# Half row factors and q copies tied behind weight splits, state-space steps in another order, the last feed-forward tile half by half

## The chip, the cores and the metric

The kernel runs on one core of one Trainium2 chip. The metric is the device time of one execution in microseconds (us), smaller is better. TensorE (PE in the rows, its weight loads PEld), VectorE (DVE), ScalarE (ACT), GpSimd (POOL) and SyncE (SP) each work through their own instruction list in order; what one needs from another it waits for at a semaphore.

## The reference

Two layers of a hybrid block on x of 256 tokens by 1024 features, all in fp32. Cut to what matters here:

```
h = rmsnorm(x, attn_norm_g)
gm_u, gm_v, ssm_z, ssm_xbc, ssm_dt, q, k, v, gates = split(h @ w_in)
y_a = gelu(gm_u) * (causal w_s applied to rmsnorm(gelu(gm_v)))          # spatial gating
y_b = rmsnorm((ssd_scan(conv(ssm_xbc), softplus(ssm_dt)) ) * silu(ssm_z))  # 16 heads of 64, chunks of 128
y_c = rmsnorm(softmax(q1 k1) v - lam * softmax(q2 k2) v)                 # 4 heads, two score maps each
g = sigmoid(gates)                                                       # three branches
x = x + (g_a*(y_a@w_a) + g_b*(y_b@w_b) + g_c*(y_c@w_c)) @ w_out
up = causal_conv3(rmsnorm(x) @ w_up);  gate, val = split(up)             # width 2816 each
x = x + (silu(gate) * val) @ w_down
```

In the scan a chunk's output is decay-masked scores times inputs within the chunk, plus what the state before it carries in.

## The kernel before

**Weights.** All weights come as one stream of 1 MB blocks over SP's queue into `raw` (3 buffers). `AHEAD` = 4 halves ahead of their use each half of a block (128x1024) is split in two: ScalarE copies it, rounded, into `whi` (L232), and VectorE writes what the rounding lost into `wlo` (L235, five buffers of each). A product is three matmuls (`mm3`, L277 to L279): high by high, high by low, low by high. `tok_group` makes an output of 256 tokens by 512 columns with matmuls of 512 columns, `feat_half` and the down projection with 256.

**Order.** The main line calls the products one after the other: q, k, the convolution inputs, v, z, the spatial branch, then for each branch the gate product and the branch product (`g_a`, `b_a`, `g_c`, `b_c`, `g_b`, `b_b`), the out projection, and 22 tile pairs of the feed-forward block with their down projection (blocks of two tiles). Small work runs beside it as generators that `tick()` steps a little after every half block, each at a rate: `norm_factors` (the row factors of an rmsnorm: squares, a sum over features by matmul `ss`, a power on POOL `r`, then `rh`, half of it, for the gates' tanh, and a row form `row`), `ssd` (rate `SSD_RATE`) and the attention. The Tile scheduler then lays the instructions of each engine in one list by priority; `tc.high_priority` moves work ahead, and `tc.issue_after(ins)` keeps work behind a given instruction.

**State-space steps.** `ssd` goes through a table, `order`. For chunk i and head group g, `decay(i, g)` makes the decay matrix in place of the buffer `seg` (eight Relu on ScalarE at L857, one Exp at L864), `masked(i, g)` multiplies it with scores and mask (VectorE, L870); `carried(g)` makes `ce` (Exp on ScalarE L846, a product on VectorE L847); `products(q)` is 24 small matmuls into `y` (L884, L886) which read two `seg` and one `ce`; `gated(q)` and `parts(q)` turn `y` into the operand of `b_b`; `factor` sums its squares (`yss`). `seg`, `ce` and other wide tiles share `NS4` = 18 buffers.

**Attention.** For a head: `sc` (scores, PE), maximum (VectorE), Exp (ScalarE, `pe`), combination (VectorE), `wt` (transposes on PE), `wT` (their copy by ScalarE, L660), `po` (PE).

**End of the feed-forward block.** `gather(j)` adds the two parts of an up tile (ScalarE L1092, VectorE L1093), `hidden(j)` does the causal convolution (L747, L752), silu (L1111), the product (L1112) and the split into `act` (ScalarE L345 high part, VectorE L347 low part). Tiles 20 and 21 feed the last down block, in which the accumulators `acc` get finished and x is updated.

Of the kernel before, what the change touches and what calls it, by code (L numbers as in the profile page):

```python
# [26 lines left out]
NFT = FFN // P  # L27
# [3 lines left out]

MIX = ("q", "k", "x4", "x5", "v", "x0", "x1", "z0", "z1", "x2", "x3", "z2", "z3", "g", "u0", "u1")

NS4, NS2, NWB, AHEAD = 18, 7, 5, 4
HP = 200


# [2 lines left out]
ROW_WAIT = 4  # L40
WARM = 11
SEG_ACT = 8
XT_RATE, SSD_RATE, ATT_RATE = 0.8, 0.95, 1.45
ATTN_IN_RATE, SSD_IN_RATE, GATE_RATE = 0.6, 0.5, 0.7


# [83 lines left out]
def block_kernel(ctx: ExitStack, tc: tile.TileContext, x, wstream, wdt, rows, prol, pcols, gains, gmw, consts, out):  # L130
    nc = tc.nc
# [5 lines left out]
    sm = ctx.enter_context(tc.tile_pool(name="sm", bufs=2))  # L137
# [9 lines left out]
    def s2(name, shape, dt=F32):  # L147
        return sm.tile(shape, dt, tag="s2", name=name, bufs=NS2)
# [51 lines left out]
    stream = {"i": 0, "raw": None}  # L200
    ready = deque()

    def load_half():
        i, hf = divmod(stream["i"], 2)
        parts = 1
        if hf == 0:
            raw = wpool.tile([P, BLK], F32, tag="raw", name=f"raw{i}", bufs=3)
            if i == 0:

                for q in range(4):  # L210
                    cs = slice(q * 512, (q + 1) * 512)
# [12 lines left out]
        src = stream["raw"][:, hf * HB : (hf + 1) * HB]
        hi = wpool.tile([P, HB], F32R, tag="whi", name=f"whi{i}_{hf}", bufs=NWB)
        lo = wpool.tile([P, HB], F32R, tag="wlo", name=f"wlo{i}_{hf}", bufs=NWB)
        for q in range(parts):
            cs = slice(q * HB // parts, (q + 1) * HB // parts)
            if i == 0:
                for k in (4 * hf + 2 * q, 4 * hf + 2 * q + 1):  # L230
                    scaled_tile(k, 0, *hT0)
            split = nc.scalar.activation(hi[:, cs], src[:, cs], AF.Copy)  # L232
            if i < 2:
                stream["first"] = split.ins
            nc.vector.tensor_tensor(lo[:, cs], src[:, cs], hi[:, cs].bitcast(F32), op=ALU.subtract)  # L235
        stream["i"] += 1
        ready.append((hi, lo))

# [144 lines left out]
    def norm_factors(name, res, later):  # L383


        tot = None
        for b in range(4):
            sq = s2(f"{name}_sq{b}", [P, 2, S])
            with tc.issue_after(stream["first"]):
                nc.scalar.activation(sq, x_sb[:, 2 * b : 2 * b + 2, :], AF.Square)  # L390
            if b:
                nc.vector.tensor_tensor(sq, sq, tot, op=ALU.add)
            tot = sq
        nc.vector.tensor_tensor(tot[:, 0, :], tot[:, 0, :], tot[:, 1, :], op=ALU.add)
        yield
        yield
        t = ps(f"{name}_ss")
        for i in range(2):
            nc.tensor.matmul(t[:, i : i + 1], tot[:, 0, i * P : (i + 1) * P], ones, start=True, stop=True)
        ss = sm.tile([P, 2], F32, tag="nss", name=f"{name}_s", bufs=2)  # L400
        nc.vector.tensor_copy(ss, t[:, 0:2])
        r = rsqrt_mean(ss, 2, 1.0 / D, f"{name}_r")
        rh = sm.tile([P, 2], F32, tag="rhalf", name=f"{name}_rh", bufs=2)
        nc.vector.tensor_scalar(rh, r[:, 0:2], 0.5, None, op0=ALU.mult)
        res.update(r=r, rh=rh)
        for _ in range(later):
            yield
        t2 = ps(f"{name}_rb")
        for i in range(2):
            nc.tensor.matmul(  # L410
                t2[:, i * P : (i + 1) * P], r[:, i : i + 1].to_broadcast([P, P]), ident, start=True, stop=True
            )
        row = sm.tile([P, S], F32, tag="rrow", name=f"{name}_row", bufs=1)
        nc.vector.tensor_copy(row, t2[:, 0:S])
        res.update(row=row)

    def hT_pair(name):
        return (
# [27 lines left out]
    for l in range(L):  # L446
# [3 lines left out]
        nf = {}  # L450
# [5 lines left out]
        def evac_qk(c0):  # L456
            def f(i, o):
                nc.scalar.activation(qk[i][:, c0 : c0 + 512], o, AF.Identity, scale=nf["r"][:, i : i + 1])

            return f  # L460

        nf_side = add_side(norm_factors(f"an{l}", nf, ROW_WAIT), 1)
        q_out = {}
        tok_group(f"q{l}", h_act, 8, q_out.__setitem__)
        r_in, rh_in = nf["r"], nf["rh"]

        def q_evac():
            for i in range(2):
                evac_qk(0)(i, q_out[i])

        pc, rw, gw, sub_g, ws = lc or layer_constants(l)

# [356 lines left out]
        def ssd():  # L829
# [88 lines left out]
            def factor():  # L918
# [7 lines left out]
                ry.append(rsqrt_mean(ss, 2, 1.0 / D, f"ry{l}"))  # L926

            order = (
                (decay, 0, 0), (masked, 0, 0), (carried, 0), (decay, 1, 0), (masked, 1, 0), (products, 0),
                (decay, 0, 1), (gated, 0), (products, 1), (masked, 0, 1), (parts, 0), (gated, 1), (carried, 1),  # L930
                (decay, 1, 1), (parts, 1), (masked, 1, 1), (products, 2), None, (gated, 2), (products, 3),
                (parts, 2), (gated, 3), None, (parts, 3), None, (factor,),
            )
            for e in order:
                if e:
# [55 lines left out]
        def branch(nm, y_act, nk, first, before, between=None):  # L991
            gts = []
            for n in range(2):
                gt = s4(f"gt{l}_{nm}_{n}", [P, 2, 512])
                gts.append(gt)
                tok_group(
                    f"g{l}_{nm}_{n}", h_act, 8,
                    lambda i, o: nc.scalar.activation(gt[:, i, :], o, AF.Tanh, scale=rh_in[:, i : i + 1]),
                )
            finish(before)  # L1000
            for n in range(2):
                cs = slice(512 * n, 512 * n + 512)
# [12 lines left out]
                tok_group(f"b{l}_{nm}_{n}", y_act, nk, evac, between if n == 1 else None)
# [22 lines left out]
        for kh in range(2):  # L1038
            for t2 in range(4):
                whi, wlo = next_half()  # L1040
                for m in range(2):
                    t = 2 * t2 + m
                    o = po[t2][:, m * S : (m + 1) * S]
# [16 lines left out]
        act, outs, us, ys, hm = {}, {}, {}, {}, []  # L1060
# [20 lines left out]
                    )  # L1081
                yield

        def gather(j):

            o = outs.pop(j)
            if j < MERGE:
                us[j] = normed(o[0], nff["row"], f"fu{l}_{j}")
                return
            us[j] = u = s2(f"fu{l}_{j}", [P, 2, S])  # L1090
            for m in range(2):
                nc.scalar.activation(u[:, m, :], o[m][:, S : 2 * S], AF.Copy)  # L1092
                nc.vector.tensor_tensor(u[:, m, :], o[m][:, 0:S], u[:, m, :], op=ALU.add)  # L1093

        def hidden(j):

            if j % 2 == 0:
                ys[0] = s4(f"fy{l}_{j}", [P, 2, 2, S])
                act["tile"] = s4(f"act{l}_{j}", [P, 4, S], F32R)
            u, y, a = us.pop(j), ys[0], act["tile"]  # L1100
            for m in range(2):
                t = 2 * j + m
                conv(u[:, m, :], y[:, m, j % 2, :], PC_FW + 3 * t, PC_FB + t, 3, pc)
            act[j] = (a[:, j % 2, :], a[:, 2 + j % 2, :])
            if j >= NFT - 2:
                js = slice(j % 2, j % 2 + 1)
            elif j % 2 == 1:
                js = slice(0, 2)
            else:
                return  # L1110
            nc.scalar.activation(y[:, 0, js, :], y[:, 0, js, :], AF.Silu)  # L1111
            nc.vector.tensor_tensor(y[:, 1, js, :], y[:, 0, js, :], y[:, 1, js, :], op=ALU.mult)  # L1112
            split_T(a[:, js, :], a[:, 2 + js.start : 2 + js.stop, :], y[:, 1, js, :])
# [5 lines left out]
        for kind, j in ffn_order():  # L1119
            if kind == "down" and not acc:  # L1120
                acc.extend(ps(f"acc{l}_{b}") for b in range(4))
            if kind == "up":
# [20 lines left out]
                if j:  # L1143
                    hidden(j - 1)
                if j == NFT - 1:
                    gather(j)
                    hidden(j)
            elif j < NFT // 2 - 1:
                for kk in range(2):
                    half = next_half()  # L1150
# [106 lines left out]
```

## Time and profile before

| what | value |
|---|---|
| time, median of 3 runs | 949.3 us (948.8 to 950.59) |
| the profiled execution | 949.31 us, of which the span is 947.5 us |
| PE busy | 935.9 us, 99% of the span |
| PEld, DVE, ACT, POOL busy | 89%, 77%, 63%, 4% |
| granted clock of TensorE | 0.999 of full speed |
| moved by DMA | 171.70 MB, 181 GB/s in the mean |

The profiled execution is within 0.01 us of the median, so terms read from its rows can be taken off the median as they are. A busy PE is not one at its peak: matmuls are pipelined, each is drawn some 0.39 us long where they start 0.23 us apart. So what a wait costs is read from start to start.

### The profile page before, as it was taken

To read this page: it belongs to the slowest core of one execution; us is meant where nothing else is said; L and a number is where in the kernel's file an instruction comes from. 1 tells how busy PE (TensorE), PEld (TensorE's weight loads), DVE (VectorE), ACT (ScalarE), POOL (GpSimd) and SP (SyncE) were. 2 spreads that over 40 slices of the span, in tenths; PEclk is the share of its full clock that TensorE was granted. 3 is DMA by queue.
4 is the path that set the end of the run, shared out by engine and by line. 5 is a ranking of instruction groups with operands and counts; after the bars stand their busy time and mean duration, and the time that the engine had idled before them with its cause. 6 is when DMAs were issued, how large, how long until landed. Compare 5 with 4: busy or idle time off the path is not lost.

```text
span 947.5 us, 15508 instructions
## 1 busy us (share of the span) xinstructions
PE 935.9 (99%) x6179; PEld 840.4 (89%) x6179; DVE 726.7 (77%) x1126; ACT 595.0 (63%) x924; POOL 37.2 (4%) x44
## 2 busy tenths in 40 slices
PE   8999999999999999999999999999999999999998
PEld 5899987888899999999989998878888999999997
DVE  6798668876568987877778974878856789787775
ACT  6575588854456856666667655878544567566663
POOL 1020010010000000000001000101000000000000
PEclk9999999999999999999999999999999999999999
DMA  9645473544644555555544555734455545455541
GB/s 335 245 172 178 177 265 131 178 152 174 208 173 152 204 184 178 178 185 193 189 177 146 179 178 167 255 127 162 148 204 183 178 169 188 178 179 186 196 152 45
DMA packets 29143, 171.70 MB, mean 181 GB/s; under 512 B 5232, under 2 KB 6544, under 8 KB 9616
## 3 DMA queue, kind: packets, MB, share of 16 engines
q1 hardware_dynamic: 27712, 166.48, 49.7%
q0 software_dynamic: 1216, 4.23, 1.5%
q8 instruction: 48, 0.79, 0.3%
q14 instruction: 23, 0.19, 0.1%
q10 hardware_dynamic: 144, 0.02, 0.0%
HBM read 169.63 MB, written 1.08 MB: 180 GB/s over the span
## 4 chain that ended last, share of the span: by engine, by line
PE 89%; ACT 5%; DVE 4%; DMA 1%; issue 1%; POOL 0%; SPq 0%; ACTq 0%; POOLq 0%
PE up L298 10%; PE up L299 5%; PE acc L278 4%; PE acc L277 4%; PE acc L279 4%; PE xbc L279 2%; PE xbc L278 2%; PE xbc L277 2%; PE up L277 2%; PE up L278 2%; PE up L279 2%; ACT whi L232 2%; DVE wlo L235 2%; PE wo L278 2%; PE z L279 2%; PE z L277 2%
## 5 line engine op out<-in xcount | busy, mean ns | idle before, releaser
L235 DVE TENSOR_TENSOR wlo<-raw,whi 128x1024 fp32r<-128x1024 f32 (+1 forms) x310 | 376.8, 1220 | 134.6 <-ACT whi L232 134.0
L232 ACT ACTIVATE whi<-raw 128x1024 fp32r<-128x1024 f32 (+1 forms) x310 | 324.2, 1050 | 242.5 <-PE up L302 37.2
L298 PE MATMUL up<-hm,whi 128*128 128x512 f32 x420 | 150.2, 396 | 0.0
L299 PE MATMUL up<-hm,wlo 128*128 128x256 f32 x420 | 117.8, 280 | 0.0
L278 PE MATMUL acc<-act,whi 128*128 128x256 f32 x352 | 99.3, 283 | 0.6 <-DVE act L347 0.6
L279 PE MATMUL acc<-act,wlo 128*128 128x256 f32 x352 | 99.1, 283 | 0.0
L277 PE MATMUL acc<-act,whi 128*128 128x256 f32 x352 | 98.3, 284 | 0.3 <-ACT act L345 0.3
L298 PEld LDWEIGHTS up<-hm,whi 128*128 128x128 f32 x420 | 79.0, 188 | 16.3
L752 DVE SCALAR_TENSOR_TENSOR fy<-fu,pc,fy 128x254 f32<-128x254 f32 (+1 forms) x176 | 80.8, 481 | 12.3 <-ACT fy L747 10.7
L299 PEld LDWEIGHTS up<-hm,wlo 128*128 128x128 f32 x420 | 79.4, 189 | 2.0
L747 ACT ACTIVATE fy<-fu,pc 128x256 f32<-128x256 f32 x88 | 51.1, 593 | 36.6 <-DVE fu L1093 32.1
L278 PEld LDWEIGHTS acc<-act,whi 128*128 128x128 f32 x352 | 67.3, 191 | 1.5 <-DVE act L347 0.8
L277 PEld LDWEIGHTS acc<-act,whi 128*128 128x128 f32 x352 | 66.6, 191 | 0.8 <-ACT act L345 0.7
L279 PEld LDWEIGHTS acc<-act,wlo 128*128 128x128 f32 x352 | 67.3, 191 | 0.0
L277 PE MATMUL up<-f_hi,whi 128*128 128x256 f32 x224 | 63.7, 284 | 0.0
L278 PE MATMUL up<-f_lo,whi 128*128 128x256 f32 x224 | 63.4, 283 | 0.0
L279 PE MATMUL up<-f_hi,wlo 128*128 128x256 f32 x224 | 63.4, 283 | 0.0
L277 PE MATMUL xbc<-h_hi,whi 128*128 128x256 f32 x192 | 55.7, 290 | 0.0
L279 PE MATMUL xbc<-h_hi,wlo 128*128 128x256 f32 x192 | 54.3, 283 | 0.0
L278 PE MATMUL xbc<-h_lo,whi 128*128 128x256 f32 x192 | 54.3, 283 | 0.0
L278 PEld LDWEIGHTS up<-f_lo,whi 128*128 128x128 f32 x224 | 43.0, 192 | 0.0
L279 PEld LDWEIGHTS up<-f_hi,wlo 128*128 128x128 f32 x224 | 43.0, 192 | 0.0
(312 smaller groups left out, 2212.3 us busy)
## 6 DMA issues: line engine op xcount, KB each, us to landing
raw<-in_wstream SPq DMA_DIRECT2D x152, 1024.0 KB, 4.8
seg<-scr POOLq DMA_DIRECT2D x8, 512.0 KB, 6.7
rows<-in_rows SPq DMA_DIRECT2D x2, 648.0 KB, 5.8
x_sb<-in_x SPq DMA_DIRECT2D x4, 256.0 KB, 4.7
raw<-in_wstream SPq DMA_DIRECT2D x4, 256.0 KB, 4.8
raw<-in_wstream SPq DMA_DIRECT2D x2, 512.0 KB, 6.6
out_x<-x_sb SPq DMA_DIRECT2D x8, 128.0 KB, 1.8
gmw<-in_gmw SPq DMA_DIRECT2D x2, 256.0 KB, 5.6
```

Of the source, the lines that this page charges most:

```text
L232: split = nc.scalar.activation(hi[:, cs], src[:, cs], AF.Copy)
L235: nc.vector.tensor_tensor(lo[:, cs], src[:, cs], hi[:, cs].bitcast(F32), op=ALU.subtract)
L277: nc.tensor.matmul(o, a_hi, b_hi, start=start, stop=False)
L278: nc.tensor.matmul(o, a_hi, b_lo, start=False, stop=False)
L279: nc.tensor.matmul(o, a_lo, b_hi, start=False, stop=stop)
L298: nc.tensor.matmul(o, whi[:, ks], hk.rearrange("p a t -> p (a t)"), start=k == 0, stop=False)
L299: nc.tensor.matmul(o_a, a_lo, b_hi, start=False, stop=False)
L747: nc.scalar.activation(y, u, AF.Identity, bias=pcl[:, bcol : bcol + 1], scale=pcl[:, wcol + taps - 1 : wcol + taps])
L752: nc.vector.scalar_tensor_tensor(y[:, d:], u[:, : S - d], pcl[:, w : w + 1], y[:, d:], op0=ALU.mult, op1=ALU.add)
```

## The change

The half row factor `rh` is made at the end of `norm_factors`, after the row form, and issued after the latest `wlo` of that moment (`stream["low"]`); the two copies of the q product out of PSUM are issued after the latest `whi` (`stream["last"]`). The table of state-space steps is put in another order, its rate is lowered, and the wide tiles get a nineteenth buffer. The last feed-forward tile is gathered half by half inside `hidden`, and this call stands in a block of high priority.

```
-NS4, NS2, NWB, AHEAD = 18, 7, 5, 4
+NS4, NS2, NWB, AHEAD = 19, 7, 5, 4
-XT_RATE, SSD_RATE, ATT_RATE = 0.8, 0.95, 1.45
+XT_RATE, SSD_RATE, ATT_RATE = 0.8, 0.85, 1.45
...
             split = nc.scalar.activation(hi[:, cs], src[:, cs], AF.Copy)
+            stream["last"] = split.ins
...
-            nc.vector.tensor_tensor(lo[:, cs], src[:, cs], hi[:, cs].bitcast(F32), op=ALU.subtract)
+            low = nc.vector.tensor_tensor(lo[:, cs], src[:, cs], hi[:, cs].bitcast(F32), op=ALU.subtract)
+            stream["low"] = low.ins
...
         r = rsqrt_mean(ss, 2, 1.0 / D, f"{name}_r")
-        rh = sm.tile([P, 2], F32, tag="rhalf", name=f"{name}_rh", bufs=2)
-        nc.vector.tensor_scalar(rh, r[:, 0:2], 0.5, None, op0=ALU.mult)
-        res.update(r=r, rh=rh)
+        res.update(r=r)
...
         nc.vector.tensor_copy(row, t2[:, 0:S])
-        res.update(row=row)
+        rh = sm.tile([P, 2], F32, tag="rhalf", name=f"{name}_rh", bufs=2)
+        with tc.issue_after(stream["low"]):
+            nc.vector.tensor_scalar(rh, r[:, 0:2], 0.5, None, op0=ALU.mult)
+        res.update(row=row, rh=rh)
...
         def q_evac():
-            for i in range(2):
-                evac_qk(0)(i, q_out[i])
+
+            with tc.issue_after(stream["last"]):
+                for i in range(2):
+                    evac_qk(0)(i, q_out[i])
...
             order = (
-                (decay, 0, 0), (masked, 0, 0), (carried, 0), (decay, 1, 0), (masked, 1, 0), (products, 0),
...
+                (decay, 0, 0), (masked, 0, 0), (carried, 0), (decay, 1, 0), (masked, 1, 0), (decay, 0, 1),
+                (products, 0), (masked, 0, 1), (carried, 1), (gated, 0), (products, 1), (decay, 1, 1), (gated, 1),
+                (masked, 1, 1), (parts, 0), (parts, 1), (products, 2), None, (gated, 2), (products, 3), (parts, 2),
+                (gated, 3), (parts, 3), (factor,),
             )
...
-        def gather(j):
+        def gather(j, ms=(0, 1)):
...
-            u, y, a = us.pop(j), ys[0], act["tile"]
+            u, y, a = us.get(j), ys[0], act["tile"]
             for m in range(2):
+                if j == NFT - 1:
+                    gather(j, (m,))
+                    u = us[j]
...
                 if j == NFT - 1:
-                    gather(j)
-                    hidden(j)
+
+                    with tc.high_priority(HP):
+                        hidden(j)
```

How the lists of the engines change is shown at three places. The lists of SP and POOL stay as they are.

**Start of layer 0, VectorE** (`an0_ss` is the sum for the row factors, `an0_rp` its power from POOL, `an0_rh` the half factor, `wlo2_0` the low part of the first half block of the k product). Before:

```order
L401 COPY an0_s_228<-an0_ss_225 128x2
L404 TENSOR_SCALAR an0_rh_234<-an0_rp_232 128x2
L235 TENSOR_TENSOR wlo2_0_164<-raw2_161,whi2_0_163 128x1024
L235 TENSOR_TENSOR wlo2_1_192<-raw2_161,whi2_1_191 128x1024
L235 TENSOR_TENSOR wlo3_0_210<-raw3_207,whi3_0_209 128x1024
```

And with the change:

```order
L403 COPY an0_s_228<-an0_ss_225 128x2
L236 TENSOR_TENSOR wlo2_0_164<-raw2_161,whi2_0_163 128x1024
L236 TENSOR_TENSOR wlo2_1_192<-raw2_161,whi2_1_191 128x1024
L236 TENSOR_TENSOR wlo3_0_210<-raw3_207,whi3_0_209 128x1024
L236 TENSOR_TENSOR wlo3_1_235<-raw3_207,whi3_1_234 128x1024
```

The half factor no longer stands ahead of `wlo2_0`; it now comes after `wlo5_0`, fourteen rows further on.

**The same place, ScalarE** (`qk0_0` and `qk0_1` are the copies of the q product). Before:

```order
L232 ACTIVATE whi2_1_191<-raw2_161 128x1024
L458 ACTIVATE qk0_0_107<-q0_0_110,an0_rp_232 128x512
L458 ACTIVATE qk0_1_108<-q0_1_111,an0_rp_232 128x512
L232 ACTIVATE whi3_0_209<-raw3_207 128x1024
L232 ACTIVATE whi3_1_236<-raw3_207 128x1024
L232 ACTIVATE whi4_0_287<-raw4_285 128x1024
L232 ACTIVATE whi4_1_316<-raw4_285 128x1024
```

And with the change:

```order
L232 ACTIVATE whi2_1_191<-raw2_161 128x1024
L232 ACTIVATE whi3_0_209<-raw3_207 128x1024
L232 ACTIVATE whi3_1_234<-raw3_207 128x1024
L232 ACTIVATE whi4_0_285<-raw4_283 128x1024
L461 ACTIVATE qk0_0_107<-q0_0_110,an0_rp_232 128x512
L461 ACTIVATE qk0_1_108<-q0_1_111,an0_rp_232 128x512
L232 ACTIVATE whi4_1_314<-raw4_283 128x1024
```

The two copies moved behind three splits, the third of which is of block 4.

**State-space stage of layer 0, PE** (`g0_a_1` is the last gate product of branch a, `y0_0` the first state-space product, `po0_0` the first attention output, `b0_a` the product of branch a). Before, from the middle of `y0_0`, whose first four matmuls stand fifteen rows earlier:

```order
L277 MATMUL g0_a_1_1_1630<-whi23_1_1593,h0_hi_105 128x512
L884 MATMUL y0_0_1721<-seg0_1_0_1471,xdt0_1_903 64x128 x2
L886 MATMUL y0_0_1721<-ce0_0_1609,prev0_904 64x128 x2
L884 MATMUL y0_0_1721<-seg0_0_0_1469,xdt0_0_902 64x128 x2
L884 MATMUL y0_0_1721<-seg0_1_0_1471,xdt0_1_903 64x128 x2
L886 MATMUL y0_0_1721<-ce0_0_1609,prev0_904 64x128 x2
L278 MATMUL g0_a_1_1_1630<-wlo23_1_1594,h0_hi_105 128x512
L279 MATMUL g0_a_1_1_1630<-whi23_1_1593,h0_lo_106 128x512
L666 MATMUL po0_0_1779<-va0_109,wT0_0_1678 128x128
```

And with the change:

```order
L279 MATMUL b0_a_0_1_1775<-whi24_0_1633,yahi0_274 128x512
L280 MATMUL b0_a_0_1_1775<-wlo24_0_1634,yahi0_274 128x512
L281 MATMUL b0_a_0_1_1775<-whi24_0_1633,yalo0_275 128x512
L889 MATMUL y0_0_1794<-seg0_0_0_1469,xdt0_0_902 64x128 x2
L889 MATMUL y0_0_1794<-seg0_1_0_1471,xdt0_1_903 64x128 x2
L891 MATMUL y0_0_1794<-ce0_0_1609,prev0_904 64x128 x2
L889 MATMUL y0_0_1794<-seg0_0_0_1469,xdt0_0_902 64x128 x2
L889 MATMUL y0_0_1794<-seg0_1_0_1471,xdt0_1_903 64x128 x2
L891 MATMUL y0_0_1794<-ce0_0_1609,prev0_904 64x128 x2
L663 MATMUL wt0_1_1807<-cst_78,pe0_1_0_1615 128x128 x3
```

The group stands in one piece, behind `po0_0` and the first twelve matmuls of `b0_a`. The later groups move likewise: `y0_1` from inside `b0_a` to behind the first twelve matmuls of `g0_c`, `y0_2` and `y0_3` to the start and the end of `b0_c`.

**The same stage, ScalarE, ahead of the last attention copy** `wT0_3` (`ysq` is the square of a finished state-space part, `osb` the scaled attention output). Before:

```order
L846 ACTIVATE ce0_1_1980<-seg0_1_1_1475 128x1024
L660 ACTIVATE wT0_2_1922<-wt0_2_1918 128x384
L232 ACTIVATE whi28_0_1937<-raw28_1935 128x1024
L897 ACTIVATE ysq0_1_1956<-xT0_0_278 128x512
L857 ACTIVATE seg0_1_1_1475<-seg0_1_1_1475,acum0_268 128x128 x2
L232 ACTIVATE whi28_1_1964<-raw28_1935 128x1024
L670 ACTIVATE osb0_1500<-po0_2_1958,rs0_2_1818 128x128 x2
L857 ACTIVATE seg0_1_1_1475<-seg0_1_1_1475,acum0_268 128x128 x6
L232 ACTIVATE whi29_0_1997<-raw29_1995 128x1024
L660 ACTIVATE wT0_3_1987<-wt0_3_1983 128x384
L864 ACTIVATE seg0_1_1_1475<-seg0_1_1_1475 128x1024
```

And with the change:

```order
L665 ACTIVATE wT0_2_1906<-wt0_2_1902 128x384
L851 ACTIVATE ce0_1_1872<-seg0_1_1_1475 128x1024
L862 ACTIVATE seg0_1_1_1475<-seg0_1_1_1475,acum0_266 128x128 x3
L232 ACTIVATE whi28_1_1956<-raw28_1919 128x1024
L862 ACTIVATE seg0_1_1_1475<-seg0_1_1_1475,acum0_266 128x128 x4
L675 ACTIVATE osb0_1500<-po0_2_1950,rs0_2_1813 128x128 x2
L862 ACTIVATE seg0_1_1_1475<-seg0_1_1_1475,acum0_266 128x128
L869 ACTIVATE seg0_1_1_1475<-seg0_1_1_1475 128x1024
L232 ACTIVATE whi29_0_1986<-raw29_1984 128x1024
L665 ACTIVATE wT0_3_1976<-wt0_3_1972 128x384
```

The Exp of the last `seg` moved ahead of the split of block 29 and of `wT0_3`. The copy `wT0_2` now stands ahead of `ce`, and the split `whi28_0` and the square stand further up.

**End of the feed-forward block of layer 0, VectorE** (`fu0_21` is the gathered last tile, `act0_20` holds tiles 20 and 21, `wlo78_0` belongs to the q product of layer 1). Before:

```order
L235 TENSOR_TENSOR wlo77_0_4832<-raw77_4829,whi77_0_4831 128x1024
L347 TENSOR_TENSOR act0_20_4803<-fy0_20_4802,act0_20_4803 128x256
L752 SCALAR_TENSOR_TENSOR fy0_20_4802<-fu0_21_4814,pc0_252,fy0_20_4802 128x255 x2
L752 SCALAR_TENSOR_TENSOR fy0_20_4802<-fu0_21_4814,pc0_252,fy0_20_4802 128x254 x2
L235 TENSOR_TENSOR wlo77_1_4860<-raw77_4829,whi77_1_4859 128x1024
L1112 TENSOR_TENSOR fy0_20_4802<-fy0_20_4802 128x256
L235 TENSOR_TENSOR wlo78_0_4890<-raw78_4887,whi78_0_4889 128x1024
L347 TENSOR_TENSOR act0_20_4803<-fy0_20_4802,act0_20_4803 128x256
```

And with the change:

```order
L757 SCALAR_TENSOR_TENSOR fy0_20_4802<-fu0_20_4776,pc0_250,fy0_20_4802 128x254
L236 TENSOR_TENSOR wlo77_0_4832<-raw77_4829,whi77_0_4831 128x1024
L757 SCALAR_TENSOR_TENSOR fy0_20_4802<-fu0_21_4814,pc0_250,fy0_20_4802 128x255
L1122 TENSOR_TENSOR fy0_20_4802<-fy0_20_4802 128x256
L757 SCALAR_TENSOR_TENSOR fy0_20_4802<-fu0_21_4814,pc0_250,fy0_20_4802 128x254
L236 TENSOR_TENSOR wlo77_1_4860<-raw77_4829,whi77_1_4859 128x1024
L1122 TENSOR_TENSOR fy0_20_4802<-fy0_20_4802 128x256
L349 TENSOR_TENSOR act0_20_4803<-fy0_20_4802,act0_20_4803 128x256 x2
L236 TENSOR_TENSOR wlo78_0_4890<-raw78_4887,whi78_0_4889 128x1024
```

Both low parts of `act` now stand ahead of `wlo78_0`, and the one of tile 20, which stood ahead of `wlo77_1`, behind it. On PE the last down block before ran twelve matmuls with tile 20, then four with the high part of tile 21 and only then one with its low part; with the change the high part of tile 21 is used by the fourth matmul and the low part by the seventh, and the second needs the low part of tile 20. At the end of layer 1 PE's list stays as it was.

## Rows read from the trace of the kernel before

**Rows 1.** The head of the page: the busy time of each engine with its share of the span and its instructions, and the clock that TensorE was granted in 40 slices of the span, in tenths.

```profile
PE 935.9 (99%) x6179; PEld 840.4 (89%) x6179; DVE 726.7 (77%) x1126; ACT 595.0 (63%) x924; POOL 37.2 (4%) x44
...
PEclk9999999999999999999999999999999999999999
```

**Rows 2.** The view of waits, PE alone: who waited for whom, us in all, how often, the longest.

```profile
PE y L884 <- DVE seg L870: 2.4, 2, 1.8
...
PE k L278 <- DVE wlo L235: 1.2, 1, 1.2
...
PE acc L278 <- DVE act L347: 0.6, 1, 0.6
```

**Rows 3.** Timelines of PE, VectorE, POOL and ScalarE at the start of layer 0; columns as in the timeline: start in us, length in us, engine, line, operation, output <- inputs, partitions x elements, count, and in brackets the idle time before it with what ended it.

```profile
19.16 0.62 PE L277 MATMUL k<-whi,h_hi 128*128 128x512 f32 x2
20.94 0.50 PE L278 MATMUL k<-wlo,h_hi 128*128 128x512 f32 x1 [1.16 <-DVE wlo L235]
...
18.31 0.16 DVE L401 COPY an_s<-an_ss 128x2 f32<-128x2 f32 x1 [0.88 <-PE an_ss L399]
19.58 0.17 DVE L404 TENSOR_SCALAR an_rh<-an_rp 128x2 f32<-128x2 f32 x1 [1.11 <-POOL an_rp L341]
19.66 5.75 DVE L235 TENSOR_TENSOR wlo<-raw,whi 128x1024 fp32r<-128x1024 f32 x4
...
18.84 0.71 POOL L341 TENSOR_TENSOR an_rp<-an_r,mhalf 128x2 f32<-128x2 f32 x1
...
24.11 2.01 ACT L232 ACTIVATE whi<-raw 128x1024 fp32r<-128x1024 f32 x2 [1.36 <-DMA raw<-in_wstream]
32.51 0.69 ACT L458 ACTIVATE qk<-k,an_rp 128x512 f32<-128x512 f32 x1 [6.39 <-PE k L279]
```

**Rows 4.** Timeline of PE in the state-space stage of layer 0, around the first `y`.

```profile
156.94 0.44 PE L884 MATMUL y<-seg,xdt 128*64 128x128 f32 x4
157.31 0.93 PE L609 MATMUL sc<-kT,qT 64*128 64x128 f32 x8
...
160.12 0.39 PE L279 MATMUL g_a<-whi,h_lo 128*128 128x512 f32 x1
160.35 0.39 PE L277 MATMUL g_a<-whi,h_hi 128*128 128x512 f32 x1
162.50 0.44 PE L884 MATMUL y<-seg,xdt 128*64 128x128 f32 x4 [1.76 <-DVE seg L870]
...
163.74 0.50 PE L278 MATMUL g_a<-wlo,h_hi 128*128 128x512 f32 x1
```

**Rows 5.** Timelines of POOL, VectorE and ScalarE in the same stretch.

```profile
153.07 1.53 POOL L430 TENSOR_TENSOR gmw<-gmw,cst 128x512 f32<-128x512 f32 x1 [25.10 <-DMA gmw<-in_gmw]
...
153.36 1.79 DVE L737 TENSOR_TENSOR gmy<-gmy,uT 128x512 f32<-128x512 f32 x1
...
160.09 1.23 DVE L235 TENSOR_TENSOR wlo<-raw,whi 128x1024 fp32r<-128x1024 f32 x1 [1.90 <-ACT whi L232]
161.23 1.22 DVE L870 TENSOR_TENSOR seg<-seg,cbm 128x1024 f32<-128x1024 f32 x1
...
155.18 1.06 ACT L846 ACTIVATE ce<-seg 128x1024 f32<-128x1024 f32 x1 [3.12 <-DVE gmy L737]
...
159.96 1.04 ACT L864 ACTIVATE seg<-seg 128x1024 f32<-128x1024 f32 x1
```

**Rows 6.** Timelines of PE and VectorE at the same place of layer 1.

```profile
628.33 0.39 PE L277 MATMUL g_a<-whi,h_hi 128*128 128x512 f32 x1
629.38 0.44 PE L884 MATMUL y<-seg,xdt 128*64 128x128 f32 x4 [0.66 <-DVE seg L870]
...
621.34 0.68 DVE L737 TENSOR_TENSOR gmy<-gmy,uT 128x512 f32<-128x512 f32 x1
```

**Rows 7.** Timelines of ScalarE and PE later in the state-space stage of layer 0, up to the last attention output.

```profile
167.95 1.06 ACT L232 ACTIVATE whi<-raw 128x1024 fp32r<-128x1024 f32 x1 [1.65 <-PE b_a L279]
...
178.69 1.06 ACT L846 ACTIVATE ce<-seg 128x1024 f32<-128x1024 f32 x1 [0.45 <-PE b_a L278]
...
186.41 0.47 ACT L660 ACTIVATE wT<-wt 128x384 f32<-128x384 f32 x1
...
178.73 0.49 PE L658 MATMUL wt<-cst,pe 128*128 128x128 f32 x3
...
186.98 0.45 PE L666 MATMUL po<-va,wT 128*128 128x128 f32 x2
```

**Rows 8.** Timelines of PE, VectorE and ScalarE at the last down block of layer 0.

```profile
470.38 0.28 PE L278 MATMUL acc<-act,whi 128*128 128x256 f32 x1
...
471.76 0.73 PE L277 MATMUL acc<-act,whi 128*128 128x256 f32 x4
473.05 0.38 PE L278 MATMUL acc<-act,whi 128*128 128x256 f32 x1 [0.55 <-DVE act L347]
...
470.27 0.42 DVE L1112 TENSOR_TENSOR fy<-fy 128x256 f32<-128x256 f32 x1
471.43 1.23 DVE L235 TENSOR_TENSOR wlo<-raw,whi 128x1024 fp32r<-128x1024 f32 x1 [0.74 <-ACT whi L232]
472.57 0.42 DVE L347 TENSOR_TENSOR act<-fy,act 128x256 fp32r<-128x256 f32 x1
...
467.46 1.06 ACT L232 ACTIVATE whi<-raw 128x1024 fp32r<-128x1024 f32 x1
```

More of the change, by code (lines that the diff above doesn't have):

```diff
@@ L464, in block_kernel @@
         tok_group(f"q{l}", h_act, 8, q_out.__setitem__)
-        r_in, rh_in = nf["r"], nf["rh"]
+        r_in = nf["r"]
         def q_evac():
-            for i in range(2):
-                evac_qk(0)(i, q_out[i])
+            with tc.issue_after(stream["last"]):
+                for i in range(2):
+                    evac_qk(0)(i, q_out[i])
         pc, rw, gw, sub_g, ws = lc or layer_constants(l)
@@ L928, in ssd @@
             order = (
-                (decay, 0, 0), (masked, 0, 0), (carried, 0), (decay, 1, 0), (masked, 1, 0), (products, 0),
-                (decay, 0, 1), (gated, 0), (products, 1), (masked, 0, 1), (parts, 0), (gated, 1), (carried, 1),
-                (decay, 1, 1), (parts, 1), (masked, 1, 1), (products, 2), None, (gated, 2), (products, 3),
-                (parts, 2), (gated, 3), None, (parts, 3), None, (factor,),
+                (decay, 0, 0), (masked, 0, 0), (carried, 0), (decay, 1, 0), (masked, 1, 0), (decay, 0, 1),
+                (products, 0), (masked, 0, 1), (carried, 1), (gated, 0), (products, 1), (decay, 1, 1), (gated, 1),
+                (masked, 1, 1), (parts, 0), (parts, 1), (products, 2), None, (gated, 2), (products, 3), (parts, 2),
+                (gated, 3), (parts, 3), (factor,),
             )
@@ L997, in branch @@
                     f"g{l}_{nm}_{n}", h_act, 8,
-                    lambda i, o: nc.scalar.activation(gt[:, i, :], o, AF.Tanh, scale=rh_in[:, i : i + 1]),
+                    lambda i, o: nc.scalar.activation(gt[:, i, :], o, AF.Tanh, scale=nf["rh"][:, i : i + 1]),
                 )
@@ L1082, in renorm @@
                 yield
-        def gather(j):
-            o = outs.pop(j)
+        def gather(j, ms=(0, 1)):
+            o = outs[j]
             if j < MERGE:
@@ L1089, in gather @@
                 return
-            us[j] = u = s2(f"fu{l}_{j}", [P, 2, S])
-            for m in range(2):
+            if 0 in ms:
+                us[j] = s2(f"fu{l}_{j}", [P, 2, S])
+            u = us[j]
+            for m in ms:
                 nc.scalar.activation(u[:, m, :], o[m][:, S : 2 * S], AF.Copy)
@@ L1099, in hidden @@
                 act["tile"] = s4(f"act{l}_{j}", [P, 4, S], F32R)
-            u, y, a = us.pop(j), ys[0], act["tile"]
+            u, y, a = us.get(j), ys[0], act["tile"]
             for m in range(2):
+                if j == NFT - 1:
+                    gather(j, (m,))
+                    u = us[j]
                 t = 2 * j + m
```

## The prediction

> **What bounds the kernel now.** The page's first two parts come first: PE is busy for 935.9 us, 99% of the span, and the granted clock is full in all forty slices [rows 1], at 0.999 in the mean. So no clock is to be won back, and the kernel ends earlier only where PE stands still or does extra work. The view of waits says where it stands: on three instructions that this change touches it waits for `y`, for the k product and for `acc` [rows 2]. These idle times understate the loss, since a matmul is drawn 0.39 us long while the next starts 0.23 us after it (160.12 to 160.35, [rows 4]). I therefore take each loss from start to start.
>
> **Start of layer 0.** Two k matmuls start from 19.16 on; the third could start at 19.16 + 2 x 0.23 = 19.62 and starts at 20.94, 1.32 late. It waits for `wlo`, which runs from 19.66 (the first of four, 1.2 us each) because VectorE stood 1.11 us for POOL's power, only to make the half factor [rows 3]. With the change `wlo2_0` follows the copy of the sum directly: from 18.47 to 19.69. The matmul starts some 0.1 late. Gain 1.2 us; bounds 0 (rival a) and 1.3.
>
> What moved there costs nothing. The half factor is read by the gates only, over 100 us later; it now stands behind `wlo5_0`. Of the two q copies, behind `whi4_0`: ScalarE had to wait 1.36 us for the landing of block 4 and splits it at 24.11, so the copies run at about 25.1 to 26.4, 5.5 us later than before, and `whi4_1` behind them some 1.3 later. Block 4 is first needed when the k product is done, and k's copy starts at 32.51 [rows 3], or 31.3 when PE is 1.2 earlier. That leaves 4 us for `wlo4_1`, even behind the small rows that moved ahead of it. The PSUM buffers of q are not asked for before that either: eight rotate, and the next product after k is the one that takes them.
>
> **State-space stage of layer 0.** PE's last gate matmul is at 160.35; `y` would start at 160.58, and some 0.08 later for the change from one matmul shape to another (an estimate, from the matmul behind the group, drawn 0.50 long at 163.74 where 0.39 is usual). It starts at 162.50 [rows 4], 1.84 late, behind the mask of `seg` on VectorE (161.23, 1.22 us), and that behind a `wlo`, the Exp on ScalarE (159.96) and the whole chain of `ce`. ScalarE had stood 3.12 us before `ce`, put down to VectorE's `gmy` [rows 5]: the buffer for `ce` came free only then. The nineteenth buffer takes this wait away, the Relu and the Exp no longer stand behind a split, and the mask stands ahead of a `wlo`. Taking off the 3.12 alone, the mask ends at 159.3. And `y` stands later: behind two gate matmuls, `po` and twelve of `b_a`, that is 160.58 + 0.46 + 0.6 + 12 x 0.227 = 164.4. Five us of margin; the wait goes. Also gone is one of two interruptions: `y` was cut in 4 matmuls (156.94 to 157.31) and 20 (162.50 to 163.74); in one piece it saves about 0.1 to 0.15, an estimate from the same row [rows 4]. Gain 1.95; bounds 1.0 (rival b) and 2.1.
>
> The other groups of `y` keep their 24 matmuls, so they cost the same at another place. What they move past is `po` and `wt` of the attention. The tightest is the last head: ScalarE copies `wT` at 186.41 to 186.88 and PE's `po` begins at 186.98 [rows 7], 0.1 of margin. Now an Exp of 1.05 us stands ahead of that copy, and PE comes at 186.98 - 1.95 = 185.03. Against that, the chain starts earlier: `y0_1` (1.5 us, as 0.37 + 1.24 less the second interruption, [rows 4]) no longer stands ahead of the `wt` of head 2, which so goes from 178.73 to 178.73 - 1.95 - 1.5 = 175.3. ScalarE's `ce` then follows its copy at about 176.2 where it was at 178.69 [rows 7]. From `ce` to the last copy took 7.7 us; now a split, a copy and a square lie elsewhere (1.0 + 0.4 + 0.5) and the Exp comes in: 6.9. The copy would be due at 183.1, but needs its own `wt`, at 183.3, so it ends near 184.3. Margin 0.7 us. I take no wait; up to 1.0 if ScalarE comes no earlier to `ce`.
>
> **The same in layer 1.** The start at 629.38 follows a matmul at 628.33: 1.05 less 0.23 and 0.08 is 0.74. That it is 1.1 smaller is VectorE's `gmy`: 0.68 here [rows 6], 1.79 in layer 0, where POOL worked on `gmw` [rows 5]. With the interruption saved: gain 0.9; bounds 0.5 and 1.0. The POOL work stays where it was, and if it now stretches `ce` by 1.1 that lies within the five us.
>
> **End of layer 0.** Four matmuls from 471.76 on would be followed at 472.24; the next starts at 473.05 [rows 8], 0.81 late. It needs the low part of tile 21 (472.57), which stood behind `wlo78_0` (471.43), and this behind a buffer that PE gave back. Now it stands ahead of it, but PE asks for it ten matmuls earlier, and for the low part of tile 20 at the second matmul of the block, 470.38. Price of VectorE's list: it gets `wlo77_1` done at 469.8 (split by ScalarE after 467.46, when its buffer comes free), the product 0.34, the low part of tile 20 0.34: 470.5. Late by 0.1. The high part of tile 21 is then ready at 470.6 (needed 470.62) and its low part at 471.0 (needed 470.98). A gain of 0.7; bounds 0.1 (wlo77_1 half a us later) and 0.8. The first add into x comes earlier with it, and nothing of layer 1 waits there: `wlo78_0` is late by some 0.5 us for a product that starts after the 48 matmuls of this block. The end of layer 1 keeps its order: 0.
>
> **Sum.** 1.2 + 1.95 + 0.9 + 0.7 = 4.75, against the profiled execution's 949.31 (and the median of 949.3): **944.6 us**. The same sum with the lower bounds that lie in the terms themselves (0.9, 1.8, 0.5, 0.1) is 3.3, thus 946.0; with the upper ones 5.2, thus 944.1, and 943.6 when as much again as the spread below the median (0.5) is allowed for.
>
> **Rivals.**
>
> (a) *POOL first.* In layer 0 `gmy` began 0.29 us after POOL's `gmw` and ended 0.55 us after it, taking 1.79 [rows 5] where 0.68 is the rule [rows 6]: VectorE stood while POOL ran. At the start `wlo2_0` moves into the time in which POOL makes the power (18.84 to 19.55, [rows 3]). If POOL goes first there, `wlo2_0` cannot start before 19.55, as now, and the 1.2 us are not won: 945.8. Against it: VectorE is done with the sum's copy at 18.47, before POOL can begin. The Trainium skill, "SBUF — State Buffer", section "SBUF: two separate sides", has a rule for this: VectorE with two SBUF inputs and a GpSimd operation share a port pair under an exclusive lock; who starts first keeps it for the whole instruction and the other fully blocks. The stretched `gmy` agrees with it (1.79 beside 0.68). By that rule, and with VectorE first, it is POOL's power that waits, which only the q copies and the row form need, much later.
>
> (b) *The last attention copy becomes the wait.* ScalarE reaches `ce` no earlier than before, because the splits ahead of it wait for PE to give back a buffer, as one did for 1.65 us at 167.95 [rows 7]. Then `po` waits until 178.69 + 6.9 + 0.5 = 186.1, 1.0 us in layer 0: 945.6. If the split that now stands between the Relu waits for 1.65 as well, in both layers, 3.3 more: 948.9. For it: the margin of before was 0.1.
>
> (c) *The gaps open again elsewhere.* The weights arrive only as fast as DMA brings them, ScalarE waited 1.36 us for a landing [rows 3], and PE running ahead would meet them later. Then the time stays at 948 to 949.3. Against it: over the whole trace no PE wait of any size is for a split that waited for a landing, but for the first ones.
>
> (d) *Slower.* PE and ScalarE wait for each other in the state-space stage, at every head: PE for `wT`, ScalarE for a weight buffer that the halted product holds. Eight copies in the two layers; from 0.8 us late at each (a split that waits 1.65 ahead of the copy would do) all that is gained and 1.9 us more are lost: above 951.2. For it is only that `wT` and `po` stand as close as in (b); against it that the other three heads have more matmuls between.
>
> **How the numbers follow.** The forecast 0.67 (943.6 to 946.0), (a) 0.06, (b) 0.16, (c) 0.07, (d) 0.04. A measurement of this kernel tells about 0.2%, 1.9 us: faster is below 947.4, slower above 951.2. Of (b) three quarters lie below 947.4: faster 0.67 + 0.06 + 0.12 = 0.85, same 0.04 + 0.07 = 0.11, slower 0.04. The range reaches from 943.6 to 947.4, where (a) and most of (b) are inside.
>
> **What the next profile would show.** Right: no PE wait for `y` or for `wlo` in the k product among the first few; the third k matmul within 0.2 us of the second; VectorE's copy of the sum followed by `wlo` without idle time; ScalarE's idle time before `ce` gone; `y` in one piece of 24; the `acc` wait below 0.2. Wrong would be: a `po` matmul waiting for `wT` (b), `wlo2_0` starting after 19.5 or lasting 1.9 us (a), `acc` waiting for the low part of tile 20 by more than 0.5, or a PE wait that the view of before does not have.

## The result and the profile after

The change takes 944.36 us in the median of 4 runs (943.87 to 944.54), beside 949.63 for the kernel before in the same series; the ratio is 0.9943 with a 95% interval of 0.9926 to 0.9961. A second series gave 944.76 us and 0.9948 (0.9933 to 0.9963). So it is faster, by some 5 us; 944.6 was forecast.

The head of the page after, as in [rows 1]:

```profile
PE 935.5 (99%) x6179; PEld 840.4 (89%) x6179; DVE 726.9 (77%) x1126; ACT 595.5 (63%) x924; POOL 38.9 (4%) x44
...
PEclk9999999999999999999999999999999999999999
```

PE's busy time and clock are what they were; the span is 942.5 us, 5.0 shorter. PE does the same work with fewer pauses. The view of waits of PE, complete, as in [rows 2]:

```profile
PE warm L174 <- DVE cold L171: 1.2, 1, 1.2
PE q L280 <- DVE wlo L236: 0.7, 2, 0.4
PE q L279 <- ACT whi L232: 0.3, 1, 0.3
PE acc L279 <- ACT act L347: 0.3, 2, 0.2
```

The waits for `y`, for `wlo` in the k product and for the low part in `acc` are gone from the view. What is left lies in the first 14 us (`warm`, `q`) or was there before (`acc` for its high part).

**A measure for the parts.** When the first weights arrive differs from execution to execution: the first k matmul starts between 19.16 and 20.39 us in the twelve traces of this study, in no order that they show. Everything behind shifts with it. So the parts are compared by the stretch from the first k matmul to the start of the last matmul. Before, that is 942.75 (the row below, PE's last) less 19.16 [rows 3], or 923.59:

```profile
942.75 0.28 PE L279 MATMUL acc<-act,wlo 128*128 128x256 f32 x1
```

After, it is 937.77 less 19.35, or 918.42:

```profile
937.77 0.28 PE L281 MATMUL acc<-act,wlo 128*128 128x256 f32 x1
```

The stretch is 5.17 shorter. It came out as 918.42 again in the second profile of the change (938.54 less 20.13), so it repeats far better than the time itself.

**Start of layer 0**, the timelines that answer to [rows 3]:

```profile
19.35 0.62 PE L279 MATMUL k<-whi,h_hi 128*128 128x512 f32 x2
19.86 0.50 PE L280 MATMUL k<-wlo,h_hi 128*128 128x512 f32 x1
...
18.50 0.16 DVE L403 COPY an_s<-an_ss 128x2 f32<-128x2 f32 x1 [0.91 <-PE an_ss L401]
18.58 3.50 DVE L236 TENSOR_TENSOR wlo<-raw,whi 128x1024 fp32r<-128x1024 f32 x3
...
18.75 1.10 POOL L341 TENSOR_SCALAR an_r<-an_s 128x2 f32<-128x2 f32 x1 [17.62 <-DVE an_s L403]
19.94 1.57 POOL L343 TENSOR_TENSOR an_rp<-an_r,mhalf 128x2 f32<-128x2 f32 x1
...
24.30 1.06 ACT L232 ACTIVATE whi<-raw 128x1024 fp32r<-128x1024 f32 x1 [3.70 <-DMA raw<-in_wstream]
25.27 1.25 ACT L461 ACTIVATE qk<-q,an_rp 128x512 f32<-128x512 f32 x2
```

The third k matmul starts 0.51 after the first of two, where it was 1.78; two usual steps are 0.45, so some 0.05 is left. VectorE goes from the copy of the sum to `wlo` at once. POOL pays for it: its two small operations for the power take 1.10 and 1.57 us, where the second took 0.71 before [rows 3]. The power is ready at 21.51, not at 19.55, and the q copies, which need it, run at 25.27.

**State-space stage of layer 0**, answering to [rows 4, 5, 7]:

```profile
149.27 1.04 ACT L851 ACTIVATE ce<-seg 128x1024 f32<-128x1024 f32 x1
150.34 2.46 ACT L862 ACTIVATE seg<-seg,acum 128x128 f32<-128x128 f32 x8
153.08 1.05 ACT L869 ACTIVATE seg<-seg 128x1024 f32<-128x1024 f32 x1
...
152.54 1.79 DVE L742 TENSOR_TENSOR gmy<-gmy,uT 128x512 f32<-128x512 f32 x1
155.36 1.21 DVE L875 TENSOR_TENSOR seg<-seg,cbm 128x1024 f32<-128x1024 f32 x1
...
163.15 0.66 PE L889 MATMUL y<-seg,xdt 128*64 128x128 f32 x8
163.63 0.39 PE L891 MATMUL y<-ce,prev 128*64 128x128 f32 x4
163.85 0.61 PE L889 MATMUL y<-seg,xdt 128*64 128x128 f32 x8
164.29 0.39 PE L891 MATMUL y<-ce,prev 128*64 128x128 f32 x4
...
175.50 1.05 ACT L851 ACTIVATE ce<-seg 128x1024 f32<-128x1024 f32 x1
...
182.27 1.06 ACT L232 ACTIVATE whi<-raw 128x1024 fp32r<-128x1024 f32 x1 [0.69 <-PE g_c L281]
183.24 0.47 ACT L665 ACTIVATE wT<-wt 128x384 f32<-128x384 f32 x1
...
183.80 0.45 PE L671 MATMUL po<-va,wT 128*128 128x128 f32 x2
```

ScalarE has no idle time before `ce`, the mask of `seg` ends at 156.57, and PE comes to `y` at 163.15: 6.6 us of margin (five were worked out). The group is in one piece. The last `wT` ends at 183.71 and its `po` starts at 183.80.

**Last down block of layer 0**, answering to [rows 8]:

```profile
467.13 0.28 PE L279 MATMUL acc<-act,whi 128*128 128x256 f32 x1
467.38 0.39 PE L280 MATMUL acc<-act,whi 128*128 128x256 f32 x1
...
466.91 0.41 DVE L349 TENSOR_TENSOR act<-fy,act 128x256 fp32r<-128x256 f32 x1
467.54 0.42 DVE L349 TENSOR_TENSOR act<-fy,act 128x256 fp32r<-128x256 f32 x1 [0.21 <-ACT act L347]
...
467.08 0.42 ACT L347 ACTIVATE act<-fy 128x256 fp32r<-128x256 f32 x1 [1.38 <-DVE fy L1122]
```

The block begins at 467.13. Its second matmul needs the low part of tile 20, which VectorE writes from 466.91 to 467.32, and starts at 467.38, 0.25 after the first instead of 0.12. That 0.13 is what is left of the wait; the high part of tile 21 (ScalarE, to 467.50) and its low part (VectorE, to 467.96) are in time for the fourth and the seventh.

### The profile page after: what moved, and what is told of

It is laid out like the page before. It is cut to its first block, busy times and chain, and to the rows that moved or that the text cites. A ratio compares the mean times of both kernels' runs of the same rounds, so it can differ in the third digit from the quotient of the medians.

```text
span 942.5 us, 15494 instructions
## 1 busy us (share of the span) xinstructions
PE 935.5 (99%) x6179; PEld 840.4 (89%) x6179; DVE 726.9 (77%) x1126; ACT 595.5 (63%) x924; POOL 38.9 (4%) x44
## 4 chain that ended last, share of the span: by engine, by line
PE 95%; ACT 2%; DMA 1%; DVE 1%; issue 0%; SPq 0%; ACTq 0%
PE up L300 10%; PE up L301 5%; PE acc L279 5%; PE acc L280 5%; PE acc L281 4%; PE xbc L280 2%; PE xbc L281 2%; PE xbc L279 2%; PE up L279 2%; PE up L280 2%; PE up L281 2%; PE g_a L279 2%; PE wo L280 2%; PE z L279 2%; PE wo L279 2%; PE z L281 2%
```

## Experiments

| kernel | time, us | ratio to before (95%) | stretch, us | less than before |
|---|---|---|---|---|
| the whole change, first and second profile | 944.36, 944.76 | 0.9943 (0.9926 to 0.9961), 0.9948 (0.9933 to 0.9963) | 918.42, 918.42 | 5.17 |
| start alone | 948.79 | 0.9992 (0.9983 to 1.0001) | 922.35 | 1.24 |
| state-space stage alone | 946.80 | 0.9967 (0.9954 to 0.9979) | 920.51 | 3.08 |
| last tile alone | 949.25 | 0.9995 (0.9986 to 1.0004) | 922.69 | 0.90 |
| whole change, 18 buffers | 945.56 | 0.9950 (0.9935 to 0.9964) | 918.53 | 5.06 |
| nineteenth buffer alone | 946.74 | 0.9963 (0.9949 to 0.9977) | 920.85 | 2.74 |
| before, `gmw` later | 949.05 | 0.9987 (0.9978 to 0.9997) | 922.52 | 1.07 |
| whole change, q copies not tied | 945.92 | 0.9955 (0.9940 to 0.9970) | 919.67 | 3.92 |
| the same, `ws` made by POOL | 944.71 | 0.9948 (0.9931 to 0.9964) | 918.39 | 5.20 |
| tie of the q copies alone | 949.99 | 1.0003 (0.9993 to 1.0012) | 923.59 | 0.00 |

The kernel before ran beside each series and took 949.63 to 950.13 us. For one part of a microsecond the times are too coarse, as the intervals show; the stretch tells the parts apart.

**Each part alone.** The edits are the hunks of the diff: first that of `rh` and `q_evac`, then the table, `SSD_RATE` and `NS4`, then `gather` and `hidden`.

> The kernel before with one part of the change: half row factor and q copies tied behind weight splits, nothing else. If the parts act each for itself, as the prediction has it, the time falls by what the two traces show at this place, 1.05 us (xbc starts at 33.67 before, at 32.62 with the whole change): 948.2 to 948.6 us, span about 946.4, the wait of the k product for wlo gone and the waits for y (1.8 and 0.7) and for acc (0.6) as before. If a gap that is closed early opens again later when the rest is as before (the rival of gaps that move), the waits for y or acc grow by as much and the span stays at 947.5.

> The kernel before with the reordered state-space steps, the lower rate and the nineteenth buffer alone. If the parts act each for itself: 2.1 us less in layer 0 and 1.0 in layer 1, 3.1 in all, so about 946.3 to 946.6 us, span about 944.4, no wait for y, the waits of k (1.2) and acc (0.6) as before. If the gain of layer 1 comes from layer 0 running earlier, or needs the other parts, it is below 2.5.

> The kernel before with the last feed-forward tile gathered half by half at high priority, nothing else. If the parts act each for itself: 0.7 to 0.85 us less (b_b to the q and k products of layer 1: 3.13 to 3.82 and 3.98), so about 948.6 us, span about 946.7, the wait of acc for the low part below 0.2. If the tile is only in time because the stages before left VectorE ahead, acc waits for the low part of tile 20 and less than 0.3 us is won.

Measured: 1.24, 3.08 and 0.90 us, 5.22 in sum, beside 5.17 for all together. The times came out 0.2 to 0.65 us above those expected, which were reckoned from 949.3 while the kernel before took 949.79 in this series. The start won more than the expected 1.05 because that number, read from two traces, had the later first k matmul of the second in it (19.35 beside 19.16). Of the 3.08, 2.11 are won by the first out-projection matmul of layer 0, and 0.97 behind it. In each run, the waits of the other parts are where they were. Waits of PE with the start alone:

```profile
PE y L889 <- DVE seg L875: 2.4, 2, 1.8
...
PE acc L280 <- DVE act L349: 0.5, 1, 0.5
```

with the state-space stage alone:

```profile
PE k L278 <- DVE wlo L235: 1.2, 1, 1.2
...
PE acc L278 <- DVE act L347: 0.5, 1, 0.5
```

and with the last tile alone:

```profile
PE y L884 <- DVE seg L870: 2.4, 2, 1.8
...
PE k L278 <- DVE wlo L235: 1.2, 1, 1.2
```

So no gap that is closed early opens again later, and no part needs another. Of the last tile's 0.90, some 0.7 lie in the down block (0.81 of [rows 8], less the 0.13 that is left). Most of the rest lies behind it, at the matmuls for the next layer's sum of squares (`an_ss`): they start 0.38 after the q matmul ahead of them in the trace before and 0.23, the usual step, with the last tile alone. Before, VectorE's last operation on the squares ended at 487.21 and the first `an_ss` matmul started at 487.35; with the last tile alone it ended at 485.84, 0.17 ahead of `an_ss` at 486.01. That PE waited there for the squares fits these times, though no view names what it waited for.

**Place or buffer.** The prediction counted on the nineteenth buffer and on the later place of `y` together. Each was tried without the other.

```
-NS4, NS2, NWB, AHEAD = 19, 7, 5, 4
+NS4, NS2, NWB, AHEAD = 18, 7, 5, 4
```

> The whole change but with 18 wide buffers instead of 19. Theory, that the later place of the y group does it: ScalarE waits some 3 us before ce for a buffer as in the kernel before, the mask of seg ends near 161, and PE comes to y at 163 all the same, so there is no wait for y and the time stays at that of the whole change, 944.4 us within 0.6 (k product to the last matmul 918.4). Rival, that the buffer does it, as the prediction put it first: PE waits for y in layer 0 by 1 us or more and the time is 945.5 or above.

ScalarE's wait before `ce` is back, and the mask ends late; yet PE does not wait (timelines of ScalarE, VectorE and PE with 18 buffers):

```profile
154.93 1.06 ACT L851 ACTIVATE ce<-seg 128x1024 f32<-128x1024 f32 x1 [3.11 <-DVE gmy L742]
...
160.97 1.22 DVE L875 TENSOR_TENSOR seg<-seg,cbm 128x1024 f32<-128x1024 f32 x1
...
163.94 0.66 PE L889 MATMUL y<-seg,xdt 128*64 128x128 f32 x8
```

The stretch is 918.53, 0.11 from that of the whole change: the later place does it without the buffer. (The time alone, 945.56, would have pointed to the rival; but the first k matmul of the profiled execution came at 20.14, not at 19.35.) The place comes from the new table and the lower rate together, which were not tried apart. The other way round, the kernel before with 19 buffers:

> The kernel before with 19 wide buffers and nothing else. The list of PE then has y0_0 in one piece where its first four matmuls stood (156.94 of the trace before), some 3.5 us ahead of the place of the other twenty. Theory, that the place decides: ScalarE's wait before ce goes, the mask of seg ends near 158, but PE asks for it at 157, so a wait for y of 1 to 1.5 us stays in layer 0 and at most 1 us is won in all (948.5 or above). Rival, that the buffer decides: no wait for y, 2.5 us or more won (947.2 or below).

My expectation fell here. The scheduler laid `y0_0` in one piece at the early place, and PE waits there for 0.30 us only (timelines of ScalarE, VectorE, PE):

```profile
150.45 1.04 ACT L846 ACTIVATE ce<-seg 128x1024 f32<-128x1024 f32 x1
...
156.55 1.21 DVE L870 TENSOR_TENSOR seg<-seg,cbm 128x1024 f32<-128x1024 f32 x1
...
157.08 0.44 PE L884 MATMUL y<-seg,xdt 128*64 128x128 f32 x4
157.82 0.44 PE L884 MATMUL y<-seg,xdt 128*64 128x128 f32 x4 [0.30 <-DVE seg L870]
```

ScalarE starts `ce` at 150.45, as `wT` also moved behind it, so the mask ends at 157.8, only just too late; the first four matmuls of the group do not need it. 2.74 of the 3.08 us come with the buffer alone. So the two are no sum: the later place removes the wait with 1.75 us to spare, the buffer removes all but 0.30 of it, and together they leave 6.6.

**Why layer 0 lost more than layer 1.** In the kernel before, the load of layer 1's spatial weights was put behind a later weight block, which changes no list but SP's and POOL's:

```
-        nc.sync.dma_start(gw, gmw[l])
+        if l:
+            with tc.issue_after(stream["load"]):
+                nc.sync.dma_start(gw, gmw[l])
+        else:
+            nc.sync.dma_start(gw, gmw[l])
```

> The kernel before, with the load of layer 1's spatial weights behind a later weight block, so that POOL masks them (gmw) in the feed-forward block and not beside VectorE's gmy; the lists of PE, VectorE and ScalarE stay as they are. If POOL stretched gmy: gmy takes 0.68 instead of 1.79 in layer 0, the wait for y falls from 1.76 to 0.66 as in layer 1, and 1.1 us is won (948.2 to 948.7). If the difference of the layers has another cause: gmy 0.68 but the wait stays above 1.5, or gmy stays at 1.8; 949.3 to 949.8.

VectorE's `gmy` takes 0.69, and PE's wait in layer 0 is that of layer 1 (timelines of VectorE and PE):

```profile
153.45 0.69 DVE L741 TENSOR_TENSOR gmy<-gmy,uT 128x512 f32<-128x512 f32 x1
...
161.49 0.44 PE L888 MATMUL y<-seg,xdt 128*64 128x128 f32 x4 [0.66 <-DVE seg L874]
```

The stretch is 1.07 shorter. The 1.1 us that POOL held VectorE went straight to PE.

**What the tie of the q copies is worth.** The prediction gave the gain of the start to the half factor and nothing to the tie.

```
-            with tc.issue_after(stream["last"]):
-                for i in range(2):
-                    evac_qk(0)(i, q_out[i])
+            for i in range(2):
+                evac_qk(0)(i, q_out[i])
```

> The whole change without the tie of the two q copies: they stand right behind whi2_1 again, ahead of whi3_0. POOL's power, which the whole change's trace has ready at 21.5 and not at 19.55, then holds ScalarE: copies 21.5 to 22.8, whi3_0 to 23.8, wlo3_0 to 25.0, and PE needs it at 19.35 + 24 x 0.23 = 24.9. Theory, that the tie is worth next to nothing beside the move of the half factor: a wait of the k product of at most 0.3 us, time within 0.5 of the whole change. Rival, that the tie carries the gain of the start: 1 us or more is lost (945.4 or above) by a wait for wlo3_0 or later ones.

The stretch grows by 1.25, so my expectation fell and the rival's size is right, but the wait is another one (timelines of PE, VectorE, ScalarE and POOL without the tie):

```profile
26.63 1.07 PE L495 MATMUL pd<-x_sb,ws 128*32 128x256 f32 x16 [1.18 <-DVE ws L441]
...
23.88 2.36 DVE L236 TENSOR_TENSOR wlo<-raw,whi 128x1024 fp32r<-128x1024 f32 x2 [2.85 <-ACT whi L232]
26.29 0.28 DVE L441 TENSOR_TENSOR ws<-ws,gcol 128x128 f32<-128x128 f32 x1
...
21.64 1.27 ACT L461 ACTIVATE qk<-q,an_rp 128x512 f32<-128x512 f32 x2 [3.52 <-POOL an_rp L343]
...
20.03 1.57 POOL L343 TENSOR_TENSOR an_rp<-an_r,mhalf 128x2 f32<-128x2 f32 x1
```

POOL's power is slowed as in the whole change. ScalarE stands 3.52 us for it with the splits of block 3 behind the copies; VectorE stands 2.85 for those; and behind its two `wlo` stands the small product `ws`, for which PE waits 1.18 before `pd`. To test this chain, POOL made that product instead (`nc.gpsimd` for `nc.vector` in that line), still without the tie:

> The whole change without the tie of the q copies, and with the small product for ws made by POOL instead of VectorE. Theory, that the tie matters because ScalarE stands for POOL's slowed power, the splits of block 3 come late and ws stands behind them in VectorE's list: ws is ready near 24, pd no longer waits (1.18 without the tie), and from the first k matmul to the last it takes 918.4 to 918.7 instead of 919.7; time 944.0 to 945.4. If PE would have had to wait for the late splits anyway, the 1.2 us come back as a wait of k for wlo and the stretch stays at 919.5 or above.

`ws` is ready at 23.66 and `pd` follows without a wait:

```profile
25.60 1.07 PE L495 MATMUL pd<-x_sb,ws 128*32 128x256 f32 x16
...
23.26 0.40 POOL L441 TENSOR_TENSOR ws<-ws,gcol 128x128 f32<-128x128 f32 x1
```

The stretch is 918.39: all is back, though the splits are as late as without the tie. What PE lost there was the wait for `ws`, not one for the late splits. And the tie without the move of the half factor:

> The kernel before with the tie of the q copies alone; the half factor still stands ahead of wlo2_0. Theory, that the two edits of the start earn together only what the half factor holds back: VectorE still waits 1.1 us for the power, k waits 1.16 for wlo, and from the first k matmul to the last it takes 923.6 us as before; time 949.3 to 950.1. If the tie earns something by itself (splits of block 3 earlier), it is 923.2 or below.

The stretch is 923.59, to the hundredth that of the kernel before, with its three waits:

```profile
PE y L886 <- DVE seg L872: 2.4, 2, 1.8
...
PE k L279 <- DVE wlo L236: 1.2, 1, 1.2
...
PE acc L279 <- DVE act L348: 0.5, 1, 0.5
```

So the move of the half factor makes the gain, and the tie (or any other way to get `ws` past the splits) keeps it.

> The whole change once more, beside the two kernels of this series. From the first k matmul to the last matmul 918.4 us again within 0.2, whatever the first 19 us take, time 943.8 to 945.2.

It took 944.76 us, and the stretch was 918.42, as in the first profile.

## Why the prediction was right

The forecast was 944.6, the sum 4.75; the median is 944.36, and the stretch fell by 5.17. The three waits were the right ones, and each went for the reason given, but that the time lies within 0.24 is in part luck. The sum was 0.42 short of the stretch, and it was taken off 949.3, where the kernel before has a median of 949.63 in its four runs; the two errors partly cancel. The terms, as each part alone measured them:

| term | forecast | measured |
|---|---|---|
| start | 1.2 | 1.24 |
| state-space stage, both layers | 1.95 + 0.9 = 2.85 | 2.11 + 0.97 = 3.08 |
| end of layer 0 | 0.7 | 0.90 |

- *From start to start.* Taken by the idle times of [rows 2], the three losses are 1.2, 2.4 and 0.6, 4.2 in all; by starts they came to 4.75. The measured 5.17 is nearer to the starts.
- *Start.* Right in size. Wrong in one reason: "What moved there costs nothing" holds only because both edits moved together. The prediction saw that POOL's power would wait for `wlo` and that only the q copies and the row form need it; it did not follow what stands behind those copies if they stay. The runs show that to be worth 1.25 us. One sign was set too tight: the third k matmul came 0.28 after the second, not within 0.2, but the usual step alone is 0.23.
- *Rival (a)*, POOL first, did not come: `wlo` began at 18.58 and POOL at 18.75. The price fell on POOL: its operations took 1.10 and 1.57, where the same two took 0.19 and 0.71 with VectorE idle, in the run of the tie alone. The Trainium skill, "SBUF — State Buffer", section "SBUF: two separate sides", says that of a VectorE operation with two SBUF inputs and a GpSimd operation the one that starts first keeps the shared port pair for the whole instruction, and the other fully blocks. The trace agrees for the first operation, which ended at 19.85, just behind the first `wlo` (19.80). It agrees only in part for the second: that ended at 21.51, 0.57 behind the second `wlo` (20.94) and inside the third (20.86 to 22.07), which took its usual 1.22. At the fourth `wlo` VectorE paid, in both kernels: with the change it began at 21.99, after POOL's 128x512 `gmw` (21.49 to 23.22), and took 2.32 (2.34 before). So "the first of four, 1.2 us each" in the prediction holds for three of the four; only the first is used in its sum.
- *State-space stage.* Right that the wait goes and that none takes its place. Its margin for the last head's copy was wrong: 0.7 us was worked out, and the copy ended with 0.1 to spare (183.71 and 183.80), as before. From `ce` to that copy took 7.74 (175.50 to 183.24), not 6.9: the split ahead of the copy waited 0.69 for a buffer that PE gave back, which is the mechanism of rival (b). Its price did not come, as no `po` matmul waits in the view. That the place does it alone, and the buffer nearly so, was not seen; it made the forecast safer than it was argued to be. The terms came out 0.16 and 0.07 small; why is not shown.
- *POOL's part in layer 0.* The reading that 1.1 us of the wait is `gmw` is now shown (1.07).
- *End of layer 0.* The low part of tile 20 was put 0.1 late and came 0.13 late, the two parts of tile 21 within 0.1 of their forecast. The further 0.2 behind the block, most of it in front of `an_ss`, was missed: "nothing of layer 1 waits there" was too quick.
- *Rival (c)*, gaps that open again, is refuted by the three parts that add up; (d) by the absence of any wait for `wT`.

## What to carry to other kernels

Where one engine is the bound and its clock does not move, read its losses from start to start against the usual pitch, and give each its own chain; here the parts added up to within 0.05 us of the whole (5.22 and 5.17). Before a tiny instruction is moved ahead or behind, list what stands behind it in its own queue and behind the consumer's queue: a 0.2 us instruction held the bound engine for 1.2, and a tie that seems to cost nothing held the same 1.2. Compare small parts by a stretch that leaves out what varies from run to run, here the landing of the first weights.

## What the runs showed of the hardware

POOL's two operations on 128x2 elements took 0.19 and 0.71 us with VectorE idle, and 1.10 and 1.57 beside VectorE's 128x1024 subtractions. These hardly changed: the first two took 2.36 us together, with POOL at work beside them or, in the run of the tie alone, without it. Where POOL's operation was a large one (128x512) and began first, VectorE paid: a 128x512 product that began 0.3 to 0.4 us later took 1.79 instead of 0.69, and a 128x1024 subtraction that began 0.5 to 0.7 later took 2.31 to 2.34 instead of 1.22. The first k matmul started at 19.16 to 20.39 us in twelve profiled executions, while the 918 to 924 us behind it came out equal to 0.01 for the one kernel that was profiled twice.
